# A hybrid mixer and MLP layer on one core: the Strassen sums of twelve weight pairs move from accumulating transfers to VectorE, and the branch and output weights are split where they are used

## The chip, the cores and the metric

One core of a Trainium2 chip runs the whole layer. The metric is the device time of one execution in microseconds. The kernel before was timed twice, 1608.06 and 1601.01 us, median 1604.53 us. Its profile is of a third execution.

## The reference

One layer on x of shape (1, 1024, 1024), float32. A combined projection feeds a pooling mixer and a stick-breaking attention of eight heads; two gates merge them, an output projection follows, and then an MLP of width 4096. Every projection is kept at nearly float32 precision.

```python
h = rmsnorm(x, g_pre_mix)
proj = h @ w_in                                  # [u_pool | q | k | v], 512 columns each
y_pool = multiscale_pool(u_pool, w_pool_mix, pool_scale) @ w_br_pool
o_sb = stick_breaking_attention(q, k, v)         # 8 heads of 64, strictly causal
y_sb = o_sb @ w_br_sb
gates = sigmoid(h @ w_gate + b_gate)             # 2048 columns
merged = gates[:, :1024] * y_pool + gates[:, 1024:] * y_sb
x = x + rmsnorm(merged @ w_out, g_post_mix)
h2 = rmsnorm(x, g_pre_mlp)
x = x + rmsnorm(square(relu(h2 @ w_up)) @ w_down, g_post_mlp)
```

The pooling mixer takes, for four groups of 128 channels, the mean over the last 2, 4, 8 or 16 positions minus the token itself, then a 128x128 map and a scale.

## The kernel before

Activations lie with channels on the 128 partitions and tokens along the free axis, in two halves of 512 tokens. Weights come in granules of 128x1024 (512 KB), an output tile of 128 columns with its eight blocks of the inner dimension. Each float32 operand is **split**: ScalarE casts it to a rounded high part, VectorE subtracts that to get the low part, and `mm3` forms a product from three TensorE matmuls (high by high, high by low, low by high). A split of a granule thus costs a copy on ScalarE and a subtraction on VectorE.

The stages follow one another:

- `phase_in` loads x, computes the norm, the pooling input u and the values v, and writes both to DRAM (`uscr`, `vscr`).
- `phase_project` computes queries, keys and gates with the Strassen-Winograd scheme: seven half products instead of eight, for **twelve pairs** of column tiles (`PAIRS`: four of queries and keys, eight of gates). For a pair with weight quarters a11, a12 (granule g1) and a21, a22 (granule g2) it needs, beside a1 = (a11, a12) and a22, the sums s3 = a21 + a22, s1 = a11 + a21, s2 = s3 + a11 and s4 = s2 + a12. In the kernel before, `sw_sums` makes them in DRAM: for three groups of four pairs, 24 transfers of 1 MiB on POOL's queue, each sum a plain transfer followed by an accumulating one, into `swscr`. `sw_weights` loads (s2, s4) and (s1, s3) from there, in rows of L524, and splits them.
- Within that stage two generators run in the background. `weight_sums` (L1204) makes the same kind of sums for the MLP's down weights, 32 transfers of 1 MiB on POOL's queue into `wscr`, issued a few at a time after the first result of each pair. `later` (L548) advances one step after each product: it prepares the values (`vscr` to `sscr`), pools the four groups (load of u L576, window sums L583, map by TensorE into dm, results to `yscr` L609), and at last takes the **branch and output weights**: sixteen granules are loaded (`hraw`, L612), split (L615 on ScalarE, L616 on VectorE), and both halves are stored to `hscr` (L618).
- Results of a pair go to DRAM on POOL's queue (`qscr`, `gscr`). Staging tiles for all this are four buffers of 512 KB in the pool `mx`, tags m0 to m3, taken in rotation by `staged`. The first two heads' queries and keys are loaded into the same four tags (L698 to L700).
- `phase_attention` runs eight heads for two halves of the queries: scores z, a scan on VectorE (L728), transposes, products with v. Between these it advances jobs: `job_pool` (branch product of the pooled path), `job_merge`, `job_out`. Their weights come by `prep`: for the branch and output weights, two loads of ready halves from `hscr` on SP's queue (L70); for the up weights, a load, a copy and a subtraction (L73 to L75). `weights(key)` prepares one key ahead, and the tiles whi and wlo have three buffers each.
- `phase_post` merges and projects the second half, and `phase_mlp` and `down` follow; they use Strassen sums too, made on VectorE for the up weights.

PSUM has eight banks, of which seven serve the pairs' products in rotation. The order of instructions on each engine is set by a scheduler; POOL, SP, VectorE and ScalarE each work through theirs in that order, so a row that waits holds up the rows behind it.

Of the kernel before, what the change touches and what calls it, by code (L numbers as in the profile page):

```python
# [32 lines left out]
P = 128  # L33
# [19 lines left out]
class Block:  # L53
# [10 lines left out]
    def prep(self, key, g, cols=None):  # L64
        nc = self.nc
        hi = self.wp.tile([P, 1024], F32R, name="whi", tag="whi", bufs=3)
        lo = self.wp.tile([P, 1024], F32R, name="wlo", tag="wlo", bufs=3)
        if cols is not None:
            for t, scr in zip((hi, lo), self.hscr[g - O_BR]):
                nc.sync.dma_start(t[:, cols].bitcast(F32), scr[:, cols])  # L70
        else:
            raw = self.wp.tile([P, 1024], F32, name="wraw", tag="wraw", bufs=2)
            nc.sync.dma_start(raw, self.w[g])  # L73
            nc.scalar.copy(hi, raw)
            self.last_lo = nc.vector.tensor_sub(lo, raw, hi.bitcast(F32)).ins  # L75
        self.prepped[key] = (hi, lo)
# [84 lines left out]
    def build(self):  # L161
# [25 lines left out]
        self.swscr = [[dp.tile([P, 4, 512], F32, name=f"swscr{n}_{q}") for q in range(4)] for n in range(3)]  # L187
        self.vscr = dp.tile([1 + P * NK, H], F32, name="vscr")
        self.sscr = [dp.tile([P, 1024], F32, name=f"sscr{t}") for t in range(NK)]
        self.hscr = [[dp.tile([P, 1024], F32, name=f"hscr{g}_{n}") for n in range(2)] for g in range(16)]  # L190
# [39 lines left out]
    def phase_in(self):  # L230
# [114 lines left out]
        def u_out(g, ps):  # L345
            for h, d in ps:
                s = evac()
                nc.vector.tensor_mul(s, d, self.rb[h])
                self.last_u = nc.gpsimd.dma_start(self.uscr[g][:, h * H : h * H + H], s)
# [23 lines left out]
        sums = self.sw_sums()  # L373
        for g in range(3):
            u_out(g, list(enumerate(dst[g])))
            if g == 0:
                with tc.issue_after(self.last_u.ins):
                    for _ in range(8):
                        next(sums)
# [21 lines left out]
        for _ in range(16):  # L401
            with tc.issue_after(self.last_u.ins):
                next(sums)
# [50 lines left out]
        gen = v_steps(1, (1, 2, 3, 0), banks)  # L454
        first = self.sw_weights(0)
# [42 lines left out]
    def sw_sums(self):  # L498

        nc = self.nc  # L500
        for n in range(3):
            g1, g2 = (self.w[g : g + 4] for g in self.sw_granules(n))
            a11, a12, a21, a22 = (g[:, :, c : c + 512].rearrange("e p n -> p e n") for g in (g1, g2) for c in (0, 512))
            s1, s2, s3, s4 = self.swscr[n]
            for out, x, y in ((s3, a21, a22), (s1, a11, a21), (s2, s3, a11), (s4, s2, a12)):
                yield nc.gpsimd.dma_start(out, x)
                yield nc.gpsimd.dma_start(out, y, accum_op=ALU.add)

    def sw_weights(self, i):
# [7 lines left out]
        for name, parts, where in (  # L517
            ("a1", (g1,), (self.wp, "w", 3)), ("sb", (s2, s4), (pool, f"s{i % 2}", 1)),
            ("sa", (s1, s3), (self.wp, "w", 3)), ("a22", (g2[:, 512:],), (pool, f"a{i % 2}", 1, 512)),
        ):  # L520
            raw = self.wp.tile([P, 1024], F32, name="wraw", tag="wraw", bufs=2)
            at = 0
            for p in parts:
                nc.sync.dma_start(raw[:, at : at + p.shape[-1]], p)  # L524
                at += p.shape[-1]
            w[name] = self.split_weights(raw[:, :at], *where)
# [21 lines left out]
    def later(self):  # L548

        nc = self.nc  # L550
        for t in range(NK):
            pair = self.staged([P, 2, H], F32, "vpair")
# [986 lines left out]
```

## Time and profile before

| | us |
|---|---|
| median of two runs | 1604.53 |
| profiled execution | 1606.4 |
| its span, first to last instruction | 1604.7 |
| TensorE busy | 1286.0 (80%) |
| VectorE busy | 945.3 (59%) |
| ScalarE busy | 615.6 (38%) |
| GpSimd (POOL) busy | 231.2 (14%) |
| DMA, share of 16 engines: queue of SP / of POOL | 39.0% / 31.9% |

The mean granted clock of TensorE was 0.902 of full speed. Transfers moved 359.58 MB. The profile has rows with the start of an instruction, its duration, its engine and line, what it writes and reads, and in brackets how long the engine was idle before and what ended that. SPq and POOL rows named DMA_DIRECT2D are issues of transfers, not the transfers. Rows of a window list the busy time of each engine in it, the granted clock, the mean busy share of the DMA engines and the rate in GB/s.

### The profile page before, as it was taken

How to read it: one execution, taken by the hardware profiler on the slowest of the kernel's cores; microseconds unless marked ns; L12 is line 12 of the kernel's file. 1: busy time of each engine (PE TensorE's matmuls, PEld its weight loads, DVE VectorE, ACT ScalarE, POOL GpSimd, SP SyncE). 2: the span in 40 equal slices, each digit the busy share in tenths (PEclk: the TensorE clock that was granted, in tenths of full speed). 3: DMA queues.
4: the chain of work that ended last, by engine and by line, in shares of the span. 5: the costliest groups of instructions: out<-in, count | busy, mean ns of one | idle time of the engine just before them, and what ended most of it. 6: DMA issues, size and time to landing. Idle time of an engine off the chain costs nothing. (4 is left out here: it accounts for less than half of the span.)

```text
span 1604.7 us, 16545 instructions
## 1 busy us (share of the span) xinstructions
PE 1286.0 (80%) x5707; PEld 1043.0 (65%) x5707; DVE 945.3 (59%) x1299; ACT 615.6 (38%) x982; POOL 231.2 (14%) x413
## 2 busy tenths in 40 slices
PE   9955885818790200788899999999999999999998
PEld 6844663616580100677777778878887788888888
DVE  8434553304461211568976478878777756576786
ACT  6223222304230111345555246655545544334443
POOL 1313222302121111121100111002111200000100
PEclk9976997868895555899999999999999999999999
DMA  5999999997967677676741686586655585465661
GB/s 189 290 267 258 271 338 287 289 228 236 256 229 264 224 250 245 193 221 183 234 126 67 232 318 216 186 288 213 215 184 177 189 296 196 171 216 180 235 254 53
DMA packets 126916, 359.58 MB, mean 224 GB/s; under 512 B 15024, under 2 KB 20144, under 8 KB 124560
## 3 DMA queue, kind: packets, MB, share of 16 engines
q1 hardware_dynamic: 78928, 202.77, 39.0%
q0 software_dynamic: 47760, 155.62, 31.9%
q8 instruction: 45, 0.74, 0.2%
q14 instruction: 39, 0.32, 0.1%
q10 hardware_dynamic: 144, 0.13, 0.0%
HBM read 270.39 MB, written 146.80 MB: 260 GB/s over the span
## 5 line engine op out<-in xcount | busy, mean ns | idle before, releaser
L105 PE MATMUL d<-blo,whi 128*128 128x512 f32 (+1 forms) x456 | 172.3, 378 | 0.0
L106 PE MATMUL d<-bhi,wlo 128*128 128x512 f32 (+1 forms) x456 | 171.9, 378 | 0.0
L104 PE MATMUL d<-bhi,whi 128*128 128x512 f32 (+1 forms) x456 | 168.7, 378 | 0.0
L722 PE MATMUL z<-kk,qq 128*128 128x256 f32 (+2 forms) x96 | 33.5, 358 | 90.9 <-DMA qq<-qscr 89.9
L104 PE MATMUL sw<-h_hi,whi 128*128 128x512 f32 x144 | 60.0, 418 | 54.1 <-ACT ev L416 31.5
L728 DVE TENSOR_TENSOR_SCAN T<-T,past 128x256 f32<-128x256 f32 (+3 forms) x96 | 90.0, 966 | 10.8 <-ACT T L727 9.6
L105 PEld LDWEIGHTS d<-blo,whi 128*128 128x128 f32 x456 | 85.7, 188 | 16.0
L106 PEld LDWEIGHTS d<-bhi,wlo 128*128 128x128 f32 x456 | 85.8, 188 | 15.8
L104 PEld LDWEIGHTS d<-bhi,whi 128*128 128x128 f32 x456 | 85.5, 188 | 16.1
L722 PEld LDWEIGHTS z<-kk,qq 128*128 128x128 f32 x96 | 18.3, 192 | 94.6 <-issue 90.3
L105 PE MATMUL d<-b_lo,whi 128*128 128x512 f32 x196 | 76.3, 389 | 0.0
L104 PE MATMUL d<-b_hi,whi 128*128 128x512 f32 x196 | 76.2, 389 | 0.0
L106 PE MATMUL d<-b_hi,wlo 128*128 128x512 f32 x196 | 75.6, 389 | 0.0
L616 DVE TENSOR_TENSOR hw<-hraw,hw 128x1024 fp32r<-128x1024 f32 x16 | 19.6, 1225 | 88.4 <-ACT hw L615 58.4
L104 PEld LDWEIGHTS sw<-h_hi,whi 128*128 128x128 f32 x144 | 28.9, 201 | 62.4 <-ACT ev L416 32.6
L753 DVE TENSOR_TENSOR alo<-at,ahi 128x512 fp32r<-128x512 f32 (+1 forms) x96 | 50.6, 548 | 28.2 <-ACT ahi L752 28.0
L1271 DVE TENSOR_TENSOR wlo<-slots_hi,whi 128x1024 fp32r<-128x1024 f32 x29 | 35.5, 1225 | 52.8 <-ACT whi L1269 52.7
L752 ACT CAST ahi<-at 128x512 fp32r<-128x512 f32 (+1 forms) x96 | 44.4, 482 | 54.8 <-PE at L744 37.7
L1269 ACT CAST whi<-slots_hi 128x1024 fp32r<-128x1024 f32 x29 | 30.5, 1052 | 83.2 <-PE d L105 70.2
L727 ACT ACTIVATE T<-z 128x256 f32<-128x256 f32 (+3 forms) x96 | 43.8, 496 | 42.6 <-PE z L725 25.1
L105 PE MATMUL sw<-h_lo,whi 128*128 128x512 f32 x144 | 59.3, 412 | 0.0
L106 PE MATMUL sw<-h_hi,wlo 128*128 128x512 f32 x144 | 58.0, 406 | 0.2
(416 smaller groups left out, 3573.2 us busy)
## 6 DMA issues: line engine op xcount, KB each, us to landing
wscr<-w POOLq DMA_DIRECT2D x24, 1024.0 KB, 20.9
wraw<-w SPq DMA_DIRECT2D x45, 512.0 KB, 5.4
ext_b<-ascr SPq DMA_DIRECT2D x40, 512.0 KB, 4.4
swscr<-w POOLq DMA_DIRECT2D x18, 1024.0 KB, 15.7
hscr<-hw POOLq DMA_DIRECT2D x32, 512.0 KB, 5.5
wraw<-swscr SPq DMA_DIRECT2D x48, 256.0 KB, 6.4
gt<-gscr POOLq DMA_DIRECT2D x32, 256.0 KB, 4.5
qq<-qscr SPq DMA_DIRECT2D x64, 128.0 KB, 5.0
```

Source lines behind the costliest of these rows:

```text
L104: nc.tensor.matmul(ps, wh, rh, start=first and i == 0, stop=False)
L105: nc.tensor.matmul(ps, wh, rl, start=False, stop=False)
L106: self.last_mm = nc.tensor.matmul(ps, wl, rh, start=False, stop=last and i == n - 1).ins
L616: nc.vector.tensor_sub(lo, raw, hi.bitcast(F32))
L722: m = nc.tensor.matmul(zz, qq[:, 0, tt], k[:, cols], start=True, stop=False)
L727: self.after = nc.scalar.activation(f, z[:, :n], AF.Sigmoid, scale=-1.0)
L728: nc.vector.tensor_tensor_scan(f[:, ::-1], f[:, ::-1], past[:, c : c + n][:, ::-1], 1.0 if top else tl[:, c + n : c + n + 1], ALU.mult, AL ...
L752: nc.scalar.copy(hi[:, c:], at[:, c:])
L753: nc.vector.tensor_sub(lo[:, c:], at[:, c:], hi[:, c:].bitcast(F32))
L1269: last_split[0] = nc.scalar.copy(hi, src).ins
L1271: last_split[1] = nc.vector.tensor_sub(lo, src, hi.bitcast(F32)).ins
```

## The change

Four things are edited. `sw_sums` and its DRAM tiles go: `sw_weights` loads the two granules of a pair, splits a1 and a22 from them, lets VectorE form the four sums in place (four additions of 128x512), and splits the tiles again as (s2, s4) and (s3 beside s1). The loaded tiles live longer, so a third buffer, wrawx, joins the two of wraw. The last part of `later` goes, with `hscr`: `prep` loads the columns it needs of the raw weights and splits them there, forty times (24 halves, 16 whole granules). To make room, c11, v and c22 have one buffer instead of two, `staged` uses two tags instead of four, and `later` gets two tags of its own with more steps between its loads and their use. Three down-weight sums are issued for each pair instead of four.

```diff
@@ def prep
-        if cols is not None:
-            for t, scr in zip((hi, lo), self.hscr[g - O_BR]):
-                nc.sync.dma_start(t[:, cols].bitcast(F32), scr[:, cols])
-        else:
-            raw = self.wp.tile([P, 1024], F32, name="wraw", tag="wraw", bufs=2)
-            nc.sync.dma_start(raw, self.w[g])
-            nc.scalar.copy(hi, raw)
-            self.last_lo = nc.vector.tensor_sub(lo, raw, hi.bitcast(F32)).ins
+        raw = self.wp.tile([P, 1024], F32, name="wraw", tag="wraw", bufs=2)
+        cols = slice(0, 1024) if cols is None else cols
+        nc.sync.dma_start(raw[:, cols], self.w[g][:, cols])
+        nc.scalar.copy(hi[:, cols], raw[:, cols])
+        self.last_lo = nc.vector.tensor_sub(lo[:, cols], raw[:, cols], hi[:, cols].bitcast(F32)).ins
@@ def phase_in
-        sums = self.sw_sums()
         for g in range(3):
             u_out(g, list(enumerate(dst[g])))
-            if g == 0:
-                with tc.issue_after(self.last_u.ins):
-                    for _ in range(8):
-                        next(sums)
...
-        for _ in range(16):
-            with tc.issue_after(self.last_u.ins):
-                next(sums)
@@ def sw_weights
-        g1, g2 = (self.w[g + e] for g in self.sw_granules(n))
-        s1, s2, s3, s4 = (s[:, e, :] for s in self.swscr[n])
+        raw = []
+        for g in self.sw_granules(n):
+            if next(self.raws) < 2 or self.sw_pools[1] is None:
+                t = self.wp.tile([P, 1024], F32, name="wraw", tag="wraw", bufs=2)
+            else:
+                t = self.sw_pools[1].tile([P, 1024], F32, name="wrawx", tag="wrawx")
+            nc.sync.dma_start(t, self.w[g + e])
+            raw.append(t)
+        r1, r2 = raw
+        a11, a12, a21, a22 = r1[:, :512], r1[:, 512:], r2[:, :512], r2[:, 512:]
         w = self.sw[i] = {}
+        w["a1"] = self.split_weights(r1, self.wp, "w", 3)
+        yield
         pool = self.sw_pools[i % 2]
...
+        w["a22"] = self.split_weights(a22, pool, f"a{i % 2}", 1, 512)
+        nc.vector.tensor_add(a22, a21, a22)
+        yield
+        nc.vector.tensor_add(a21, a11, a21)
+        nc.vector.tensor_add(a11, a11, a22)
+        nc.vector.tensor_add(a12, a12, a11)
+        yield
+        w["sb"] = self.split_weights(r1, pool, f"s{i % 2}", 1)
+        yield
+        w["sa"] = self.split_weights(r2, self.wp, "w", 3)
@@ def staged
-        return self.mx.tile(shape, dt, name=name, tag=f"m{self.turn % 4}")
+        return self.mx.tile(shape, dt, name=name, tag=f"m{self.turn % 2}")
@@ def later: vpair and vs take tags m2 and m3, one more step after the loads of a pair, two more after u
-        for g in range(16):
-            raw = self.staged([P, 1024], F32, "hraw")
-            nc.sync.dma_start(raw, self.w[O_BR + g])
-            yield
-            hi, lo = (self.staged([P, 1024], F32R, "hw") for _ in range(2))
-            nc.scalar.copy(hi, raw)
-            nc.vector.tensor_sub(lo, raw, hi.bitcast(F32))
-            for t, scr in zip((hi, lo), self.hscr[g]):
-                nc.gpsimd.dma_start(scr, t.bitcast(F32))
-            yield
@@ def phase_project
-            return pw.tile([P, H], F32, name=name, tag=name, bufs=2)
+            return pw.tile([P, H], F32, name=name, tag=name, bufs=1 + (name == "u"))
-            for _ in range(4):
+            for _ in range(3):
                 with tc.issue_after(done.ins):
                     next(self.wsums, None)
```

Three places show what moves. Line numbers of the changed kernel are its own, up to 22 lower.

POOL, from the end of the first projections to the first pair (vscr holds the values, vlast a small copy of them, qscr the first results, wscr the down weights' sums, swscr the pairs' sums). Before:

```order
L417 DMA vscr<-ev 128x512
L506 DMA swscr_1_151<-swscr_2_152 16x16384
L506 DMA swscr_1_155<-swscr_2_156 16x16384
L507 DMA swscr_3_149<-w 512x1x512
L507 DMA swscr_1_151<-w 512x1x512
L507 DMA swscr_1_155<-w 512x1x512
L417 DMA vscr<-ev 128x512 x3
L506 DMA swscr_3_153<-swscr_1_151 16x16384
L506 DMA swscr_3_157<-swscr_1_155 16x16384
L417 DMA vscr<-ev 128x512
L507 DMA swscr_3_153<-w 512x1x512
L507 DMA swscr_3_157<-w 512x1x512
```

With the change:

```order
L404 DMA vscr<-ev 128x512 x8
L466 DMA vlast<-vscr 64x8x1 x8
L532 DMA qscr_0_138<-qs 256x1x512
L1195 DMA wscr_0_126<-w 512x1x512
L1195 DMA wscr_1_127<-w 512x1x512
L1195 DMA wscr_2_128<-w 512x1x512
L549 DMA sscr_147<-vs 128x1024
L532 DMA qscr_2_140<-qs 256x1x512 x2
```

The stores of the values no longer stand between sums, and the first pair's first result is followed by three sums of the down weights.

VectorE, from the pooling of the fourth group (win, pq and u) to the first scans of attention (T); gt is a branch product. Before:

```order
L592 TENSOR_TENSOR win<-win,u 128x16
L597 TENSOR_TENSOR pq<-win,ph 128x1024
L604 SCALAR_TENSOR_TENSOR u<-dm,vt,win 128x512 x2
L616 TENSOR_TENSOR hw<-hraw,hw 128x1024 x4
L825 TENSOR_TENSOR gt<-gt,dbr 128x512
L616 TENSOR_TENSOR hw<-hraw,hw 128x1024 x12
L825 TENSOR_TENSOR gt<-gt,dbr 128x512
L728 SCALAR_TENSOR_TENSOR T<-T,past 128x512
```

With the change:

```order
L581 TENSOR_TENSOR win<-win,u 128x16
L586 TENSOR_TENSOR pq<-win,ph 128x1024
L593 SCALAR_TENSOR_TENSOR u<-dm,vt,win 128x512 x2
L804 TENSOR_TENSOR gt<-gt,dbr 128x512 x2
L72 TENSOR_TENSOR wlo<-wraw,whi 128x512
L707 SCALAR_TENSOR_TENSOR T<-T,past 128x512
```

The sixteen splits are gone from this place; one split of a branch weight stands there, and others stand among the scans behind it.

SP, where the fourth group's u is loaded, behind the loads of the values and of the third head's queries (qscr_2), with the change:

```order
L677 DMA qq<-qscr_2_140 64x512
L678 DMA qq<-qscr_2_140 64x512
L70 DMA wraw<-w 128x512
L563 DMA u<-uscr_137 128x1024
L679 DMA kk<-qscr_0_142 64x512 x4
L677 DMA qq<-qscr_0_138 64x512
```

The load of u keeps its place behind them; before, the loads of hraw and hscr followed it, and now the first heads' keys and queries do.

More of the change, by code (lines that the diff above doesn't have):

```diff
@@ L186, in build @@
         self.qscr = [[dp.tile([P, 2, 1024], F32, name=f"qscr{i}_{j}") for j in range(4)] for i in range(2)]
-        self.swscr = [[dp.tile([P, 4, 512], F32, name=f"swscr{n}_{q}") for q in range(4)] for n in range(3)]
         self.vscr = dp.tile([1 + P * NK, H], F32, name="vscr")
         self.sscr = [dp.tile([P, 1024], F32, name=f"sscr{t}") for t in range(NK)]
-        self.hscr = [[dp.tile([P, 1024], F32, name=f"hscr{g}_{n}") for n in range(2)] for g in range(16)]
         self.bscr = [[dp.tile([P, H], F32, name=f"bscr{e}_{h}") for h in range(2)] for e in range(8)]
@@ L348, in u_out @@
                 nc.vector.tensor_mul(s, d, self.rb[h])
-                self.last_u = nc.gpsimd.dma_start(self.uscr[g][:, h * H : h * H + H], s)
+                nc.gpsimd.dma_start(self.uscr[g][:, h * H : h * H + H], s)
         d2 = [self.dps.tile([P, H], F32, name="du", tag="d") for _ in range(2)]
@@ L454, in phase_in @@
         gen = v_steps(1, (1, 2, 3, 0), banks)
+        self.raws = itertools.cycle(range(3))
         first = self.sw_weights(0)
@@ L496, in sw_granules @@
         return a, a + (4 if n == 0 else 8)
[L498 to L507, printed above, removed]
     def sw_weights(self, i):
@@ L512, in sw_weights @@
         n, e = i // 4, i % 4
-        g1, g2 = (self.w[g + e] for g in self.sw_granules(n))
-        s1, s2, s3, s4 = (s[:, e, :] for s in self.swscr[n])
+        raw = []
[8 more added lines that the diff above has]
+        a11, a12, a21, a22 = r1[:, :512], r1[:, 512:], r2[:, :512], r2[:, 512:]
         w = self.sw[i] = {}
+        w["a1"] = self.split_weights(r1, self.wp, "w", 3)
+        yield
         pool = self.sw_pools[i % 2]
[L517 to L526, printed above, removed]
-            yield
+        w["a22"] = self.split_weights(a22, pool, f"a{i % 2}", 1, 512)
[8 more added lines that the diff above has]
+        w["sa"] = self.split_weights(r2, self.wp, "w", 3)
     def staged(self, shape, dt, name):
         self.turn += 1
-        return self.mx.tile(shape, dt, name=name, tag=f"m{self.turn % 4}")
+        return self.mx.tile(shape, dt, name=name, tag=f"m{self.turn % 2}")
     def result(self, kind, f, h, t, sign):
@@ L551, in later @@
         for t in range(NK):
-            pair = self.staged([P, 2, H], F32, "vpair")
+            p = self.mx.tile([P, 2, H], F32, name="vpair", tag="m2")
             for j in range(2):
-                nc.sync.dma_start(pair[:, j, :], self.vscr[t * P + j : t * P + j + P, :])
+                nc.sync.dma_start(p[:, j, :], self.vscr[t * P + j : t * P + j + P, :])
             yield
-            e = pair[:, 0, :]
-            nc.vector.tensor_sub(e, e, pair[:, 1, :])
+            yield
+            e = p[:, 0, :]
+            nc.vector.tensor_sub(e, e, p[:, 1, :])
             e = e.rearrange("p (h x) -> p h x", h=8)
-            v = self.staged([P, 8, P], F32R, "vs")
+            v = self.mx.tile([P, 8, P], F32R, name="vs", tag="m3")
             nc.scalar.copy(v[:, :, 0:64], e)
@@ L576, in later @@
             nc.sync.dma_start(u, self.uscr[g])
+            yield
+            yield
             yield
@@ L609, in later @@
                 nc.gpsimd.dma_start(scr.bitcast(F32), t)
-        for g in range(16):
-            raw = self.staged([P, 1024], F32, "hraw")
-            nc.sync.dma_start(raw, self.w[O_BR + g])
-            yield
-            hi, lo = (self.staged([P, 1024], F32R, "hw") for _ in range(2))
-            nc.scalar.copy(hi, raw)
-            nc.vector.tensor_sub(lo, raw, hi.bitcast(F32))
-            for t, scr in zip((hi, lo), self.hscr[g]):
-                nc.gpsimd.dma_start(scr, t.bitcast(F32))
-            yield
     def run(self, gen):
```

## The prediction

> **What bounds the kernel now.** I began with the slices of the page. From its third to its seventeenth forty-microsecond slice TensorE is far from full, and for four slices around the fourteenth it is nearly empty. From slice 18 on it is full. A change can only earn much in that hole.
>
> ```profile
> PE   9955885818790200788899999999999999999998
> DMA  5999999997967677676741686586655585465661
> ```
>
> So I cut the span at the places where the work changes: the first projections (0 to 99), the twelve pairs (99 to 486), the gap to the first attention score (486 to 649), attention (to 900), the merge and output products of the second half (to 960), the MLP.
>
> ```profile
> core 0: us, PE busy (x) PEld busy (x) DVE busy (x) ACT busy (x) POOL busy (x), PEclk, DMA share, GB/s
> 99.00:486.00 387.00, 261.32 (x1027) 206.60 (x1025) 165.90 (x230) 107.25 (x150) 83.65 (x121) 0.82 0.95 267
> 486.00:649.00 163.00, 11.90 (x27) 7.39 (x27) 29.95 (x32) 19.37 (x20) 22.82 (x43) 0.53 0.73 246
> 649.00:900.00 251.00, 230.07 (x1169) 187.37 (x1169) 185.22 (x282) 123.82 (x290) 31.49 (x86) 0.98 0.53 163
> 900.00:960.00 60.00, 55.13 (x225) 42.27 (x224) 38.62 (x60) 20.19 (x35) 10.73 (x20) 0.97 0.89 335
> 960.00:1605.00 645.00, 631.44 (x2858) 523.31 (x2857) 466.99 (x608) 304.82 (x424) 55.98 (x104) 1.00 0.60 204
> ```
>
> No compute engine is busy for more than 68% of the pairs' stage, while the DMA share is 0.95: transfers bound it. In the gap nothing is busy at all: a chain of small waits. After 649 TensorE leads, with VectorE at 74% in attention. The order of a wait's cause comes from the timeline: how a pair goes when transfers are light, what happens when accumulating transfers pile up, and how the gap is filled.
>
> ```profile
> 131.13 0.79 PE L104 MATMUL sw<-h_hi,whi 128*128 128x512 f32 x1 [29.39 <-ACT ev L416]
> 364.43 0.59 ACT L651 COPY u<-sw 128x512 f32<-128x512 f32 x1 [43.31 <-DMA gscr<-u]
> 447.23 0.57 ACT L651 COPY u<-sw 128x512 f32<-128x512 f32 x1
> 467.30 0.59 ACT L651 COPY u<-sw 128x512 f32<-128x512 f32 x1 [1.31 <-PE sw L106]
> 200.00:230.00 30.00, 23.92 (x95) 18.93 (x94) 12.26 (x17) 7.27 (x10) 5.91 (x9) 0.89 0.99 361
> 330.00:360.00 30.00, 0.00 (x0) 0.00 (x0) 0.00 (x0) 0.00 (x0) 1.68 (x3) 0.54 1.13 214
> ```
>
> The copy at L651 opens every pair, so two of them in a row give a pair that TensorE paces: 467.30 - 447.23 = 20.1 us. From 330 to 360 all engines stand still: the eight accumulating sums of the down weights (L1214) that were issued just before drain, at 214 GB/s with the share at 1.13, and the result of an earlier pair waits behind them (43.31 us). Plain traffic reaches 361 GB/s at a share of 0.99.
>
> **The pairs' stage (99 to 486).** What goes: those of the twelve pairs' sums that still ran here, and part of the weight loads.
>
> ```profile
> 101.18 0.50 POOL L506 DMA_DIRECT2D swscr<-swscr  x1 [4.77 <-DMA swscr<-w]
> 155.77 1.16 POOL L507 DMA_DIRECT2D swscr<-w  x1 [2.19 <-DMA swscr<-swscr]
> L1214 POOL DMA_DIRECT2D wscr<-w x16: 1151/1891/3557, 237.8 to 397.4; - x16
> wscr<-w POOLq DMA_DIRECT2D x24, 1024.0 KB, 20.9
> wraw<-w SPq DMA_DIRECT2D x45, 512.0 KB, 5.4
> wraw<-w SPq DMA_DIRECT2D x24, 256.0 KB, 6.5
> ```
>
> The first two rows are the first and the last of nine sums of 1 MiB issued after 99: 9.4 MB, five of them accumulating (5.2 MB). A pair's loads shrink from 1.84 MB (one granule of 512 KB, a half, and four quarter-megabyte sums) to 1.05 MB, some 9 MB in all. The stage moved 267 GB/s x 387 us = 103 MB; 85 MB stay, 16.8 MB of them the sixteen accumulating transfers of L1214. At the two rates above that is 16.8/0.214 = 78 us and 68/0.361 = 189 us, **267 us** of transfers. TensorE alone needs 12 x 20.1 = 241 us. The same sum for the kernel before gives 22/0.214 + 81/0.361 = 328 us, and it took 387, because a first-in-first-out queue also stalls TensorE where the transfers come unevenly: factor 1.18. So the new stage lies between 267 and 315 us. I take 290, the middle: the stall at 131 (29.39 us, the projection's results behind the pairs' sums in POOL's queue) goes, but the query and key pairs now hold their results in two buffers instead of four, and c11, v and c22 in one each, so a result store that lands late behind three sums of 1 MiB still stops VectorE. Saving **97 us** (72 to 120).
>
> VectorE gets four additions of 128x512 for each pair, 48 in all. A 128x512 operation on loaded data takes 0.69 us in the rows further down: 33 us on an engine busy for 166 us of the stage; 199 of 290 us leaves it off the bound. If that cover were gone it would cost at most these 33 us. The sums are no longer awaited from DRAM, but the raw tiles stay occupied until the last sum is split; three tiles rotate and the load is ahead by a pair, 20 us against 5.4 us of landing, so I cost it at nothing.
>
> **The gap (486 to 649).** Its rows in order of time:
>
> ```profile
> 484.31 7.17 SPq L680 DMA_DIRECT2D v<-sscr  x8
> 511.63 0.52 SPq L576 DMA_DIRECT2D u<-uscr  x1
> 516.67 1.22 DVE L583 TENSOR_TENSOR win<-u 128x1023 f32<-128x1023 f32 x1 [30.26 <-DMA u<-uscr]
> 532.16 0.54 POOL L609 DMA_DIRECT2D yscr<-u  x1 [0.25 <-DVE u L604]
> 537.12 0.53 POOL L674 DMA_DIRECT2D ylo<-yscr  x1
> 546.73 0.77 PE L104 MATMUL dbr<-yhi,whi 128*128 128x512 f32 x1 [16.38 <-DMA whi<-hscr]
> 639.23 1.22 DVE L616 TENSOR_TENSOR hw<-hraw,hw 128x1024 fp32r<-128x1024 f32 x1 [5.98 <-ACT hw L615]
> 640.48 0.45 SPq L698 DMA_DIRECT2D qq<-qscr  x1
> 649.42 1.08 PE L722 MATMUL z<-kk,qq 128*128 128x512 f32 x2 [89.94 <-DMA qq<-qscr]
> ```
>
> Two things fill it. First the pooling of the fourth group: its load of u stands on SP behind eight loads of v and twelve of queries and keys, is issued at 511.63, and the result goes out at 532.16 and comes back from 537.12. Then sixteen rounds of load, split and store of the branch and output weights, until 639.23; only then are the four buffers free for the first heads' queries, and 9 us later the first score runs. The change removes the rounds and nothing else: in its order the u load still stands behind the same v, query and key loads. What is late next is the store of the pooled u; when it has landed (537.12 - 486 = 51 us after the last product) the first head's transfers need what they needed before, 649.42 - 640.48 = 9 us. The gap becomes 60 to 64 us, I take 62: saving **101 us**. The bounds: 90, if the branch products, which now wait for a split, come in front of the scores; 110, if the lighter traffic lands u sooner.
>
> **Attention and the stage behind it.** Here the forty fetches of ready halves become loads, splits by ScalarE and VectorE.
>
> ```profile
> 134.11 0.62 ACT L1086 CAST a0hi<-wraw 128x512 fp32r<-128x512 f32 x1 [0.97 <-DMA wraw<-w]
> 134.77 0.69 DVE L1087 TENSOR_TENSOR a0lo<-wraw,a0hi 128x512 fp32r<-128x512 f32 x1 [2.35 <-ACT a0hi L1086]
> L75 DVE TENSOR_TENSOR wlo<-wraw,whi 128x1024 fp32r<-128x1024 f32 x17 | 20.8, 1221 | 7.6 <-ACT whi L74 7.6
> L74 ACT CAST whi<-wraw 128x1024 fp32r<-128x1024 f32 x17 | 17.9, 1053 | 18.1 <-PE d L105 9.8 <-DMA wraw<-w 6.0 <-PE du L105 2.3
> ```
>
> Three of the forty run in the gap. In attention there are thirteen halves and eight whole tiles: VectorE 13 x 0.69 + 8 x 1.22 = 18.7 us, ScalarE 13 x 0.62 + 8 x 1.05 = 16.5 us, on 185 and 124 of 251 us. Below nothing is not reached, above both in series, 35 us. I take **+9**: half of VectorE's share, since its scans hold TensorE for part of the stage only (230 of 251 us busy). From 900 to 960 eight halves and eight tiles add 15.3 us to VectorE's 38.6 of 60; TensorE waits 5 us there now, with the DMA share at 0.89, and half the bytes go. Bounds -5 and +15, I take **+3**. The MLP has no edit; its sums of the down weights end before attention in both.
>
> **The sum.** The profiled execution took 1606.4 us (its span 1604.7), 1.9 above the median of 1604.53. 1606.4 - 97 - 101 + 9 + 3 = **1420 us**.
>
> **A rule weighed.** The Trainium skill's page "DMA: Bandwidth & Descriptors", section "Bandwidth", gives 6.15 us or 341 GB/s for 1 MiB loaded by a software-generated transfer and no other price for one that accumulates. By it the 16.8 MB would be an estimated 49 us, not 78, the transfers 238 us, and TensorE would pace all pairs. The trace disagrees with its 214 GB/s, measured on DRAM to DRAM, where the page measured loads into SBUF.
>
> **The rivals.** (1) **TensorE paces every pair.** Accumulating transfers may be slow only because eight came in a row; now three a pair leave time for plain loads beside them. For it: the pairs from 447 on. Against: in the first pairs 8 MB a pair must move. The stage then takes 241: 1606.4 - 146 - 101 + 12 = 1371 us. (2) **The pairs' stage keeps its time**, because stores behind sums meet single buffers; for it, the 43.31 us of L651 came from exactly such a store with two buffers; against it, 18 MB less: 1420 + 97 = 1517 us. (3) **The gap keeps its time**: the change does not do what it says, since v, query and key loads and not the rounds hold the scores. Against it, the loads are all issued by 511.63 and the rounds end 9 us before the first score: 1420 + 101 = 1521 us. (4) **Slower: every split is waited for.** If SP, ScalarE and VectorE took the forty preparations in line with TensorE, 24 x (6.5 + 0.62 + 0.69) + 16 x (5.4 + 1.05 + 1.22) = 310 us: 1606.4 - 198 + 310 = 1718 us. It decides from 5 us each (198/40). Against it: seventeen splits by the same code waited 6.0 us in all for their loads.
>
> **Chances and range.** The forecast, 1385 to 1465, gets 0.72; rivals (1) 0.14, (2) 0.07, (3) 0.05, (4) 0.02. The low ends of the terms give 1606.4 - 120 - 110 - 5 = 1371; the high ends 1606.4 - 72 - 90 + 35 + 15 = 1494, which needs all four at once. I give 1374 to 1478, which takes in nearly all of the forecast and most of rival (1). A measurement of this kernel tells about 2% (32 us) from no change. All but rival (4) are faster by more: 0.97 faster, 0.01 within 2%, 0.02 slower.
>
> **What would show it.** Right: the first score near 450 us, no row of L616's kind between the last product and it, the u load of the fourth group some 26 us after the last product; the pairs' stage at a DMA share above 0.9 in its first half and pairs 20 us apart in its second; VectorE near 205 us in attention. Wrong: pairs 20 us apart from the first on (rival 1), copies of u waiting more than 20 us for a result store (2), more than 70 us from the last product to the first score (3), TensorE waiting for split weights in the branch and output products for more than a microsecond each (4).

## The result, and the profile after

The changed kernel took 1406.59 us (median of two runs) against 1604.53: a ratio of 0.877, with a 95% interval of 0.868 to 0.885. The forecast was 1420, its range 1374 to 1478. The profiled execution took 1407.21 us, its span 1405.5. The two rows of slices, to lay beside those of before:

```profile
PE   9998887899826988898989999999999999999998
DMA  5326999999965765620266668755565854656661
```

The hole in TensorE's row is now the twelfth slice and part of the thirteenth, where four stood before. The same stages by windows: pairs, gap, attention, the stage behind it, MLP.

```profile
core 0: us, PE busy (x) PEld busy (x) DVE busy (x) ACT busy (x) POOL busy (x), PEclk, DMA share, GB/s
97.00:377.00 280.00, 246.67 (x1024) 197.42 (x1023) 169.18 (x241) 97.14 (x137) 72.33 (x105) 0.95 0.94 277
377.00:438.00 61.00, 16.94 (x34) 8.60 (x33) 20.73 (x32) 6.79 (x9) 8.07 (x15) 0.53 0.73 244
438.00:684.00 246.00, 220.60 (x1128) 179.93 (x1127) 198.29 (x298) 136.46 (x305) 32.83 (x88) 0.98 0.45 130
684.00:764.00 80.00, 72.94 (x296) 58.03 (x295) 60.07 (x87) 37.76 (x61) 10.79 (x20) 0.94 0.59 205
764.00:1405.00 641.00, 628.20 (x2829) 519.98 (x2828) 462.34 (x601) 301.67 (x419) 56.19 (x104) 0.99 0.60 204
```

For all kernels below I cut each trace at the same five events: the first and the last product of the pairs, the first score, the last value product of attention, the first product of the MLP. The lengths between them, in us (the prediction's marks were round numbers near these; a "gap" below zero means that scores start before the pairs end):

| kernel | up to pairs | pairs | gap | attention | behind it | MLP | median |
|---|---|---|---|---|---|---|---|
| before | 98.9 | 385.3 | 165.2 | 241.2 | 71.5 | 642.6 | 1604.5 |
| after | 97.4 | 279.7 | 60.9 | 246.3 | 80.2 | 641.0 | 1406.6 |
| gap_part | 98.8 | 387.2 | 61.7 | 245.1 | 74.0 | 646.6 | 1516.5 |
| sums_part | 98.6 | 280.7 | 162.8 | 238.1 | 72.7 | 647.8 | 1500.1 |
| plain_sums | 98.9 | 257.9 | 63.2 | 246.4 | 80.5 | 640.0 | 1390.3 |
| no_acc_sums | 98.7 | 253.3 | 37.7 | 245.8 | 73.6 | 640.2 | 1350.9 |
| turning_tiles | 98.9 | 289.9 | 40.3 | 247.6 | 76.4 | 640.0 | 1396.9 |
| early_sums | 107.5 | 285.5 | 41.7 | 247.9 | 75.2 | 649.6 | 1408.1 |
| late_sums | 143.8 | 266.6 | 21.3 | 247.0 | 80.4 | 641.8 | 1401.8 |
| late_turning | 143.0 | 265.4 | -0.1 | 274.1 | 74.8 | 645.3 | 1405.3 |
| adds_twice | 98.4 | 316.9 | 43.3 | 247.7 | 73.2 | 648.0 | 1427.8 |
| attention_sums | 97.8 | 251.2 | 20.7 | 270.9 | 75.7 | 650.1 | 1368.4 |
| attention_turning | 98.4 | 249.6 | -0.1 | 289.5 | 80.9 | 647.5 | 1366.9 |
| spread_sums | 98.3 | 243.6 | 43.7 | 267.3 | 80.5 | 640.4 | 1375.5 |

So the change took 105.6 us from the pairs and 104.3 from the gap, and gave back 5.1 in attention and 8.7 behind it. The kernel before was timed again beside each group of later runs; its medians lay between 1604.2 and 1606.1 us, so times of different groups may be compared to within about 2 us. The length "behind it" needs care: in the kernel before (and in sums_part) the last 22 matmuls of that stage run only after the first one of the MLP, until 968.4 us; in the changed kernel (and in gap_part) none does. At 0.24 us each they are an estimated 5.3 us, counted behind attention after the change and in the MLP before it.

How the pairs go now, by the timeline of the copy that opens each (L630, L651 before): the sixth opens 50 us after the fifth; from the eighth on they are 18 to 24 us apart. What held the sixth stands in the rows behind them: six accumulating sums (L1193) go out on GpSimd's queue within 8 us, then the store of a block of values (sscr). The values have one tile for that store (vs), and ScalarE waits 19.91 us for the store to land before it casts the next block and comes to the pair's copy.

```profile
199.68 0.59 ACT L630 COPY u<-sw 128x512 f32<-128x512 f32 x1 [3.76 <-DVE qs L529]
249.59 0.59 ACT L630 COPY u<-sw 128x512 f32<-128x512 f32 x1 [0.81 <-DVE ks L529]
297.90 0.57 ACT L630 COPY u<-sw 128x512 f32<-128x512 f32 x1
319.45 0.56 ACT L630 COPY u<-sw 128x512 f32<-128x512 f32 x1
...
202.91 3.61 POOL L1193 DMA_DIRECT2D wscr<-w  x3 [0.42 <-issue]
207.05 3.59 POOL L1193 DMA_DIRECT2D wscr<-w  x3
208.94 2.26 POOL L549 DMA_DIRECT2D sscr<-vs  x1
246.90 0.62 ACT L547 CAST vs<-vpair 128x512 fp32r<-128x512 f32 x1 [19.91 <-DMA sscr<-vs]
```

And the gap, in order of time (timeline, three engines and the queue of SP together):

```profile
394.61 0.54 POOL L598 DMA_DIRECT2D yscr<-u  x1 [0.25 <-DVE u L593]
402.43 0.33 SPq L563 DMA_DIRECT2D u<-uscr  x1
409.14 1.22 DVE L572 TENSOR_TENSOR win<-u 128x1023 f32<-128x1023 f32 x1 [14.82 <-DMA u<-uscr]
424.63 0.54 POOL L598 DMA_DIRECT2D yscr<-u  x1 [0.25 <-DVE u L593]
438.01 1.16 PE L701 MATMUL z<-kk,qq 128*128 128x512 f32 x3
```

No round of load, split and store is left. The load of the fourth group's u is issued 25.3 us after the last product (402.43 - 377.1; announced: some 26), its pooling ends with the store at 424.63, and the first score follows 13 us later.

### The profile page after: what moved, and what is told of

Same layout as the page of the kernel before. It is cut to its first block, busy times and chain, and to the rows that moved or that the text cites. A ratio compares the mean times of both kernels' runs of the same rounds, so it can differ in the third digit from the quotient of the medians.

```text
span 1405.5 us, 16309 instructions
## 1 busy us (share of the span) xinstructions
PE 1279.6 (91%) x5707; PEld 1038.3 (74%) x5707; DVE 982.5 (70%) x1371; ACT 626.3 (45%) x1006; POOL 193.1 (14%) x357
## 5 line engine op out<-in xcount | busy, mean ns | idle before, releaser
L71 ACT CAST whi<-wraw 128x1024 fp32r<-128x1024 f32 (+1 forms) x57 | 49.6, 872 | 73.0 <-PE dbr L102 32.6
L72 DVE TENSOR_TENSOR wlo<-wraw,whi 128x1024 fp32r<-128x1024 f32 (+1 forms) x57 | 56.6, 994 | 27.9 <-ACT whi L71 26.5
L103 PE MATMUL d<-b_hi,wlo 128*128 128x512 f32 x196 | 74.8, 389 | 0.0
L1248 ACT CAST whi<-slots_hi 128x1024 fp32r<-128x1024 f32 x29 | 30.5, 1051 | 83.2 <-PE d L102 66.6
L732 DVE TENSOR_TENSOR alo<-at,ahi 128x512 fp32r<-128x512 f32 (+1 forms) x96 | 50.6, 548 | 20.7 <-ACT ahi L731 20.0
L1248 ACT CAST whi<-slots_lo 128x1024 fp32r<-128x1024 f32 x27 | 28.5, 1054 | 73.5 <-PE d L102 58.2
L1250 DVE TENSOR_TENSOR wlo<-slots_lo,whi 128x1024 fp32r<-128x1024 f32 x27 | 33.0, 1223 | 35.5 <-ACT whi L1248 35.3
L723 PE MATMUL at<-eye,T 128*128 128x128 f32 x288 | 47.9, 275 | 10.8 <-DVE alo L732 10.7
```

Source lines behind the costliest of these rows:

```text
L71: nc.scalar.copy(hi[:, cols], raw[:, cols])
L72: self.last_lo = nc.vector.tensor_sub(lo[:, cols], raw[:, cols], hi[:, cols].bitcast(F32)).ins
L103: self.last_mm = nc.tensor.matmul(ps, wl, rh, start=False, stop=last and i == n - 1).ins
L723: t = nc.tensor.transpose(at[:, r * P : r * P + P], a[r][:, s * P : s * P + P], self.eye)
L732: nc.vector.tensor_sub(lo[:, c:], at[:, c:], hi[:, c:].bitcast(F32))
L1248: last_split[0] = nc.scalar.copy(hi, src).ins
```

## The experiments

Two theories stood against each other at each place. Mine: the two parts are separate, transfers at two rates bound the pairs, a chain of pooling bounds the gap. Against it: the parts hide or expose each other; places in queues and buffers, not bytes, hold the pairs.

**One part alone, twice.** gap_part is the kernel before with this edit (and without the rounds in the generator):

```diff
-        if cols is not None:
-            for t, scr in zip((hi, lo), self.hscr[g - O_BR]):
-                nc.sync.dma_start(t[:, cols].bitcast(F32), scr[:, cols])
...
+        nc.sync.dma_start(raw[:, cols], self.w[g][:, cols])
+        nc.scalar.copy(hi[:, cols], raw[:, cols])
+        self.last_lo = nc.vector.tensor_sub(lo[:, cols], raw[:, cols], hi[:, cols].bitcast(F32)).ins
```

> The kernel before, with only the branch and output weights split at their use (no rounds of load, split and store ahead of attention). Theory (the two parts are separate and add): the gap loses about 104 us, attention and the stage behind it gain 14, the pairs' stage keeps its 385 us: 1606 - 104 + 14 = 1516, between 1500 and 1532. Rival A (the fourth group's load and the loads of v and queries hold the first score once the rounds are gone, because the transfers ahead are as heavy as before): the gap falls only to about 100 us, 1555. Rival B (the rounds' own traffic slowed the end of the pairs' stage): the pairs' stage falls too, below 1490.

Measured 1516.46, ratio 0.944 (0.941 to 0.947). sums_part is the other half: the changed kernel with the sixteen rounds and the fetches of ready halves put back, in the four tiles' own turn.

```diff
+            tags = [f"m{(3 * g + k) % 4}" for k in range(3)]
+            raw = self.mx.tile([P, 1024], F32, name="hraw", tag=tags[0])
...
+            hi, lo = (self.mx.tile([P, 1024], F32R, name="hw", tag=t) for t in tags[1:])
```

> The kernel after, with the sixteen rounds ahead of attention put back (branch and output weights fetched ready from DRAM again), so that only the twelve pairs' sums are changed. Theory (additive): 1407 + 104 - 14 = 1497, between 1480 and 1512, pairs' stage 280 us as in the changed kernel. Rival (the rounds are paid for only as far as transfers are congested, and with 9 MB less ahead of them they run faster): a gap of 120 us instead of 163 and 1455.

Measured 1500.12, ratio 0.935 (0.931 to 0.938). The two savings, 87.9 and 104.2, add to 192.1 where the whole change saved 197.9; the rivals of both runs are out. The table shows it stage by stage: gap_part has the pairs of before (387.2) and the gap of after (61.7), sums_part the reverse (280.7 and 162.8). The pair of runs also prices the splits in both surroundings: with them attention and the stage behind it are 3.9 and 2.5 us longer (gap_part against before), or 8.2 and 7.5 (after against sums_part), the second figure of each pair with those 22 matmuls.

**What bounds the pairs.** plain_sums makes sixteen transfers plain, no_acc_sums leaves them out (first and second diff, both in weight_sums):

```diff
-                    self.nc.gpsimd.dma_start(out[q], a, accum_op=ALU.add)
+                    self.nc.gpsimd.dma_start(out[q], a)
```

```diff
-                if add:
-                    self.nc.gpsimd.dma_start(out[q], a, accum_op=ALU.add)
-                else:
+                if not add:
                     self.nc.gpsimd.dma_start(out[q], a)
```

> The kernel after, with the sixteen accumulating transfers of the down weights' sums made plain copies of the same size and place (the down products' weights are then not the sums). Theory (two rates, 214 GB/s for accumulating and 361 for plain): 16.8 MB take 46 us instead of 78, the transfers of the pairs' stage 215 instead of 247, so TensorE paces the stage at about 250 instead of 280 us, and poolings that start earlier shorten the gap by some 5: 1372, between 1360 and 1385. Rival A (accumulating costs no more per byte): no change, 1400 to 1412. Rival B (what costs is the place in POOL's queue, a result behind 1 MiB of anything): a third of the gain at most, 1395.

> The kernel after, with the sixteen accumulating transfers of the down weights' sums left out (so these sums are not formed; the sixteen plain ones stay). Theory (transfers bound the rest of the pairs' stage): 169 us of transfers remain, TensorE paces all pairs, stage about 247 us, gap 50 instead of 61: 1364, between 1350 and 1375. Rival (the single buffers of c11, v and c22 and of the value tiles hold the pairs, not the transfers): stage still above 270 us and 1395 or more.

Measured 1390.29 (0.866, 0.864 to 0.868) and 1350.92 (0.841, 0.839 to 0.844). The windows of the pairs' stage, plain_sums first, then no_acc_sums:

```profile
99.00:357.00 258.00, 241.89 (x1023) 195.68 (x1022) 173.78 (x248) 97.65 (x136) 64.36 (x104) 0.97 0.86 303
```

```profile
99.00:352.00 253.00, 242.12 (x1030) 196.37 (x1029) 186.33 (x270) 103.58 (x143) 57.82 (x98) 0.97 0.71 254
```

The last three columns are the clock, the DMA share and the rate. The share falls from 0.94 to 0.86 and 0.71, TensorE is busy for 242 of 258 and 253 us. So transfers did bind what was left of the stage, and an accumulating one costs more than a plain one of the same size: 21.8 us of the stage for sixteen, where the two rates gave 32. That price is not spread over the sixteen. Some 16 of the 21.8 us lie between the fifth and the sixth opening copy (49.9 us apart in the changed kernel, 34.2 in plain_sums), behind the six sums of 203 us. While they move, the changed kernel's rate is 243 GB/s at a share of 1.08; in plain_sums the same stretch runs at 359 GB/s at 0.99, and the store behind them costs ScalarE 3.71 us instead of 19.91:

```profile
203.00:246.00 43.00, 34.75 (x143) 27.54 (x141) 16.85 (x22) 9.70 (x13) 11.25 (x13) 0.94 1.08 243
```

```profile
203.00:230.00 27.00, 25.38 (x103) 20.11 (x103) 16.29 (x21) 9.14 (x13) 8.48 (x13) 0.94 0.99 359
230.14 0.62 ACT L547 CAST vs<-vpair 128x512 fp32r<-128x512 f32 x1 [3.71 <-DMA sscr<-vs]
```

The total of plain_sums fell by 16 and not by the announced 34, outside the theory's range: the stage gave some 8 us less than announced, and the gap, which was to shorten by 5, stayed (63.2). It lies between theory and rival B, and the rows above bear out a part of rival B: the place behind 1 MiB transfers in GpSimd's queue matters. Leaving the sums out (no_acc_sums, inside its range) took 55.7 us, of which only 26.4 are in the pairs and 23.2 in the gap: poolings that are no longer delayed. Single buffers by themselves hold nothing, since they are the same in all three kernels; behind sums in the queue one of them, vs, turned a late landing into the longest stall of the stage. Rate, place in the queue and single tile act together there, and no run has a second vs tile to price it alone.

**What holds the gap.** In turning_tiles a group's u goes to the tile that its predecessor's ph leaves, not to the one whose store must land first:

```diff
+        tags = [0, 1, 2, 3]
         for g in range(4):
-            u = whole(0, name="u")
+            tu, t1, t2, tq = tags
+            u = whole(tu, name="u")
...
-            ph, pq = whole(3 - n, F32R, "ph"), whole(3, F32R, "pq")
+            th = t1 + t2 - n
+            tags = [th, tq, tu, n]
+            ph, pq = whole(th, F32R, "ph"), whole(tq, F32R, "pq")
```

> The kernel after, with the four tiles of the pooling groups taken in turn: a group's load of u goes to the tile of the group before's ph, which is free after its two products, and not to the tile that waits for the store of u to land. Theory (the gap is the chain of four poolings, each load held by the single tile of u until the store before it has landed): each of three loads comes 8 to 10 us earlier, the first score 15 to 25 us earlier: 1387, between 1380 and 1394. Rival (the loads are held by the place of the steps between the pairs' products, or by transfers): no change, 1402 to 1410.

Measured 1396.85 (0.870, 0.867 to 0.873): half of what was expected. SP's own waits for the four loads, of the changed kernel (in all, then between 399 and 404 us alone), and of this one:

```profile
SPq L563 <- DMA yscr<-u: 23.3, 3, 12.2
SPq L563 <- DMA yscr<-u: 2.7, 1, 2.7
```

```profile
SPq L565 <- PE dm L103: 7.3, 2, 3.9
```

The tile held the second and the third load (8.4 and 12.2 us). The fourth, the only one in the gap, waited for it for 2.7 us. It is issued at 388.01 instead of 402.43 mainly because it now stands ahead of the eight loads of values in SP's order, and the gap falls by 20.6 us. But the pairs' stage is 10.2 us longer, and the trace shows most of that: TensorE waits there for the casts of two pooled groups, 10.4 us where the changed kernel has 1.6. A group's window sums now take the tile that the store holds, so VectorE waits for the store in SP's stead. Rows of turning_tiles:

```profile
PE dm L101 <- ACT ph L589: 10.4, 2, 5.5
372.17 1.22 DVE L574 TENSOR_TENSOR win<-win 128x1022 f32<-128x1022 f32 x1 [9.00 <-DMA yscr<-u]
377.40 0.80 PE L101 MATMUL dm<-ph,wm 128*128 128x512 f32 x1 [5.46 <-ACT ph L589]
388.01 0.60 SPq L565 DMA_DIRECT2D u<-uscr  x1
388.66 10.82 SPq L663 DMA_DIRECT2D v<-sscr  x8
```

**Sums of the down weights elsewhere.** early_sums issues twelve of the thirty-two in the first projections, and two instead of three for each pair.

```diff
             u_out(g, list(enumerate(dst[g])))
+            if g == 0:
+                for _ in range(8):
+                    with tc.issue_after(self.last_u.ins):
+                        next(self.wsums)
...
+        for _ in range(4):
+            with tc.issue_after(self.last_u.ins):
+                next(self.wsums)
```

> The kernel after, with twelve of the thirty-two transfers of the down weights' sums (8 plain, 4 accumulating) issued during the first projections, and two instead of three for each pair. Theory (transfers bound the pairs' stage; the first 97 us have room at 137 GB/s): 8.4/0.361 + 4.2/0.214 = 43 us of transfers leave the stage, which becomes TensorE-paced at 255 instead of 277 us, gap 45 to 55: 1370, between 1355 and 1385. Rival (the first results stand in POOL's queue behind them, as in the kernel before at 131 us, 29 us): 1395 to 1410.

Measured 1408.06 (0.877, 0.874 to 0.881): the rival. The pairs' stage does fall to a share of 0.79, and from its first opening copy to its end it takes 254 us (263 in the changed kernel). But that copy comes at 139.06 instead of 114.37. The window of the stage, the copy, and the waits of this kernel between 100 and 160 us:

```profile
107.00:393.00 286.00, 245.47 (x1027) 197.82 (x1028) 192.18 (x280) 108.58 (x153) 66.98 (x103) 0.95 0.79 235
```

```profile
139.06 0.58 ACT L637 COPY u<-sw 128x512 f32<-128x512 f32 x1
```

```profile
POOL vscr L411 <- ACT ev L410: 45.4, 5, 20.9
ACT ev L410 <- DMA vscr<-ev: 18.9, 2, 16.5
```

The stores of the values stand behind sums in GpSimd's queue, as at 131 us in the kernel before. That waiting is a matter of the queue's order, and no sum of bytes contains it.

late_sums and late_turning were to issue all thirty-two in attention, behind each head's scores (late_turning with the tiles in turn as well).

```diff
+                for _ in range(2):
+                    with tc.issue_after(self.after.ins):
+                        next(self.wsums, None)
                 out = self.att_steps(h, g, [a[i] for i in rows[::-1]])
```

> The kernel after, with all thirty-two transfers of the down weights' sums issued in attention, two behind each of the sixteen heads' score groups, and none during the pairs. Theory (what is bound by transfers is only the pairs' stage; attention moves 130 GB/s and has room for 124 us of transfers in 246): pairs' stage 248 us and gap 41 us as in the run without accumulating sums, attention and post together +10: 1360, between 1345 and 1375. Rival (the gates' loads and stores in POOL's queue stand behind 1 MiB transfers, and the branch products hold TensorE): attention +40 or more, 1390 to 1420.

> The two edits together: sums of the down weights in attention and the pooling groups' tiles taken in turn. Theory: they add as far as poolings are still the end of the gap: late sums' time minus 10, 1350. Rival (without the sums' traffic the poolings end in time and something else, the loads of the first heads, holds the first score): same as with late sums alone.

Neither ran so. The instruction they were tied to (self.after, the last sigmoid) is ScalarE's, and it held back nothing on GpSimd; the trace of late_sums has the first eight sums at the very start:

```profile
L1195 POOL DMA_DIRECT2D wscr<-w x8: 793/1182/1595, 4.1 to 8.4; - x8
L1193 POOL DMA_DIRECT2D wscr<-w x16: 1151/1164/1250, 18.1 to 148.2; - x16
```

So these two are runs with all sums beside the first projections: 46 us are lost there (143.8 against 97.4), 13 won in the pairs, 40 in the gap; 1401.77 (0.873, 0.871 to 0.876) and, with the turned tiles, 1405.28 (0.876, 0.873 to 0.879). They say nothing on their expectations.

attention_sums does it: each sum is queued behind a store or load that GpSimd itself issues for the branch products.

```diff
-            for _ in range(3):
-                with tc.issue_after(done.ins):
-                    next(self.wsums, None)
...
-        nc.gpsimd.dma_start(self.bscr[e][h], t)
+        self.some_sums(nc.gpsimd.dma_start(self.bscr[e][h], t), 1)
```

> The kernel after, with the thirty-two transfers of the down weights' sums in attention, each queued on GpSimd behind a store or a load of the branch products there (one behind each of sixteen, two behind each of eight), and none during the pairs. Theory (the sums' transfers bind in the pairs' stage alone; attention moves 130 GB/s of 361): pairs' stage 250 us, gap 35 to 40, attention and post together no more than +12: 1352, between 1342 and 1368. Rival (the branch products' loads and stores in the same queue stand behind 1 MiB transfers, and TensorE waits for them in order): attention +40 us or more, 1385 to 1420.

> The same, with the pooling groups' tiles taken in turn as well. Theory (in the run with those tiles alone the gap fell by 21 us and the pairs' stage rose by 10, since transfers still bound it; without the sums there is nothing to give back): 5 to 20 us less than with the sums in attention alone: 1338. Rival (without the sums the poolings are early, and the loads of the first heads into the same four tiles end the gap): same time within 4 us.

Measured 1368.42 (0.852, 0.849 to 0.855) and 1366.85 (0.852, 0.849 to 0.854). They beat the changed kernel by 2.7 and 2.8%. The first lies just outside the theory's range: the pairs came as expected (251.2), the gap below it (20.7), but attention is 25 us longer and the MLP 9, where 12 were the most expected for attention and the stage behind it. Windows of attention_sums, the pairs and the two parts of attention:

```profile
98.00:349.00 251.00, 242.30 (x1034) 197.77 (x1033) 188.42 (x272) 104.87 (x144) 47.82 (x82) 0.97 0.55 189
370.00:550.00 180.00, 156.13 (x731) 125.82 (x731) 137.67 (x209) 90.47 (x214) 52.14 (x100) 0.89 1.07 313
550.00:641.00 91.00, 82.96 (x404) 67.25 (x403) 62.14 (x90) 45.90 (x93) 10.97 (x20) 0.96 0.54 147
```

The share is 0.55 in the pairs and 1.07 in the first 180 us of attention: the load on the transfers has moved there. What it costs there shows as slower products more than as waits. TensorE is busy for 239 us of attention where it was 221 in the changed kernel, for about as many matmuls (1134 and 1129), with a granted clock of 0.89 in the first 180 us where it was 0.97; its idle time grows by 6.5 us. Why the clock is lower these runs do not show. With the turned tiles the gap disappears (-0.1) and attention takes the same time back (289.5): the rival's time, within 2 us. A first score stands right behind the pairs there, but a later one waits 11 us, while SP still issues the first heads' queries, until 384:

```profile
382.29 0.76 PE L702 MATMUL z<-kk,qq 128*128 128x512 f32 x1 [11.08 <-issue]
```

The profile names no releaser for that wait, so that these loads end it, as the rival said, is likely and not shown.

spread_sums puts the first eight back to the pairs and one instead of two behind each merge product.

```diff
             done = self.result(kind, f1, 0, c11, 1.0)
+            if i < 8:
+                self.some_sums(done, 1)
...
-            self.some_sums(self.last_in, 2)
+            self.some_sums(self.last_in, 1)
```

> The kernel after, with the eight first plain transfers of the down weights' sums in the first eight pairs (one each), and the other twenty-four in attention, one behind each of the sixteen pool products' stores and one behind each of eight merge products' loads. Theory (transfers may be put wherever a stage has room; with all in attention its first 180 us had a DMA share of 1.03 to 1.08 and attention rose by 25): 8 MB at 361 GB/s fit beside the pairs, which stay at 252, gap 25, attention 258 to 264: 1360, between 1352 and 1368. Rival (the price of a transfer is the same in either place, since what the pairs lose attention gains): 1366 to 1374, no better than with all of them in attention.

Measured 1375.48 (0.858, 0.856 to 0.861), worse than either said. The pairs were never shorter (243.6), but the gap is 43.7. SP's queue shows a reason, here and in no_acc_sums. In spread_sums:

```profile
343.95 8.20 SPq L658 DMA_DIRECT2D v<-sscr  x8
354.26 0.45 SPq L677 DMA_DIRECT2D qq<-qscr  x1
382.08 0.59 SPq L677 DMA_DIRECT2D qq<-qscr  x1
```

```profile
385.62 1.30 PE L700 MATMUL z<-kk,qq 128*128 128x512 f32 x3 [22.12 <-DMA qq<-qscr]
```

All eight loads of the values go out ahead of the first heads' queries, which are issued until 382. In attention_sums five of the eight stand behind most of them, and the score comes 20.7 us after the pairs:

```profile
365.86 4.06 SPq L656 DMA_DIRECT2D v<-sscr  x5
```

A kernel with spread sums and the queries ahead of the values was not tried, so this is read from the traces.

**VectorE's additions.** adds_twice puts one more operation of the same size behind each of the 48.

```diff
         nc.vector.tensor_add(a22, a21, a22)
+        self.same(a22)
...
+    def same(self, x):
+        self.nc.vector.scalar_tensor_tensor(out=x, in0=x, scalar=1.0, in1=x, op0=ALU.mult, op1=ALU.max)
```

> The kernel after, with one more VectorE operation of 128x512 on the same tile behind each of the pairs' 48 additions (a product with one and a maximum, which changes no value). Theory (VectorE is busy 169 of 280 us in the pairs' stage and the raw weights are ahead of their use, so the additions lie beside other work): 48 x 0.68 = 33 us more of work, no more than 5 of them seen: 1402 to 1412. Rival (load, four additions and the last split are a chain that TensorE waits for in every pair): most of the 33 us appear, 1430 or more.

Measured 1427.77 (0.888, 0.885 to 0.892), 21 us more: between the theory (1402 to 1412) and its rival (1430). My theory is out. The pairs alone are 37 us longer (316.9); the gap fell by 17.6, since the fourth u was loaded at the same time as in the changed kernel (403.0 and 402.4 us) while the pairs ended later. Of the 37, 16 are TensorE's products taking longer (busy 262.5 against 246.7 us, granted clock 0.89 against 0.95) and 21 are waits. SP's waits for the tile of a raw weight from 97 to 415 us, after and then with the added operations (L496 is the load of a pair's weights):

```profile
SPq L496 <- DVE wlo L1066: 62.0, 8, 11.4
SPq L496 <- DVE s0lo L1066: 24.9, 6, 8.1
```

```profile
SPq L496 <- DVE wlo L1073: 75.8, 9, 20.3
SPq L496 <- DVE s0lo L1073: 51.3, 6, 13.2
```

The next pair's load waits for the split behind the additions, 40 us more in sum: the tile stays occupied longer and the load goes out later. The other path is direct. ScalarE's casts of the sums wait for the operation in front of them, and TensorE for these casts: 16.7 us in the changed kernel, 26.5 with the added operations. How much goes by which path no run shows; one with a fourth raw tile would.

```profile
PE sw L101 <- ACT whi L1065: 16.7, 6, 5.5
```

```profile
PE sw L101 <- ACT whi L1072: 26.5, 7, 8.2
```

## Why the prediction was right, point by point

- **Pairs, 290 forecast, 279.7 measured (bounds 267 to 315).** The bound was right: less traffic made the stage shorter, and less again made it TensorE's (253.3, 243.6; forecast 241 for TensorE alone). The number is partly luck, as errors on both sides met. The two rates gave too high a price to accumulating: 32 us for the sixteen, 21.8 in the stage. The traffic fell by more than was counted, to 277 GB/s x 280 us = 77.6 MB and not 85. Put into the same sum, it gives 16.8/0.214 + 60.8/0.361 = 247 us; the stage took 1.13 times that, before 1.18. And a factor for the whole stage hides that the largest single loss sits at one place, the store behind six sums: the kind of late store that the text named, but of the values, not of a pair's result.
- **The additions at nothing.** This step failed. They are not hidden with room to spare: doubled, they cost 21 us of the kernel and 37 of the stage, more than the 33 that the text named as the most. The first 48 are on the path as well: in the changed kernel ScalarE's casts of weights wait 13.5 us in eight waits for an addition (L507), and some of TensorE's 16.7 us stand behind these casts. What the first 48 cost by themselves was not measured. The raw tiles that "stay occupied until the last sum is split" were the very cover that I counted on.
- **The gap, 62 forecast, 60.9 measured, by the reason given, with a second one close behind.** The rounds went and nothing else did, as said; gap_part gives 61.7 by itself. There the load of the fourth u goes out 27.9 us after the last product, right behind the loads of values and queries on SP, while the store that frees its tile was issued long before, at 490.11:

```profile
490.11 0.54 POOL L605 DMA_DIRECT2D yscr<-u  x1 [0.25 <-DVE u L600]
...
513.92 0.52 SPq L572 DMA_DIRECT2D u<-uscr  x1
```

  In the changed kernel the same loads stand ahead of it. SP is through with them at 399.7, 22.6 us after the last product, and then waits 2.7 us more for the tile. The forecast did not name the tile; it set the last tenth of the 25.3 us.

```profile
399.17 0.53 SPq L70 DMA_DIRECT2D wraw<-w  x1
```

- **Attention +9 and the stage behind it +3, measured +5.1 and +8.7.** The sum (12 against 13.8, of which the 22 matmuls are some 5) is near, its parts are less so. VectorE has 198 of 246 us, near the 205 announced. Behind attention TensorE waits twice for a split, once at length, and once for the merge:

```profile
PE d L103 <- DVE wlo L72: 4.4, 2, 4.0
PE d L101 <- ACT mg_hi L826: 2.7, 1, 2.7
```

  That is 7.1 us of waits; before, it waited 4.9 us for transfers. The other part is time at work, 73.1 us where it was 66.6: the 22 matmuls more, some 5.3 us, and a granted clock of 0.94 where it was 0.98. Without these matmuls the stage is some 3.4 us longer, near the forecast of 3.
- **The rule that was weighed.** The Trainium skill's page "DMA: Bandwidth & Descriptors", section "Bandwidth", has one price for 1 MiB and no other for one that accumulates. plain_sums disagrees: the same sixteen transfers without accumulating took 16 us less of the whole and landed sooner (median of the sixteen 12.0 us from issue, with accumulating 20.8). The estimate of 49 us was worked out from the rate alone. The two figures of that row do not fit each other: 1 MiB in 6.15 us is 170 GB/s, and sixteen times 6.15 us are an estimated 98 us, so the page gives no firm price here.
- **The rivals.** TensorE did not pace every pair (rival 1): the sixth opens 50 us after the fifth. It does without the sums. Rivals 2 and 3 are out by the stages. But the mechanism of 2, a store behind sums that meets a single buffer, made the longest stall of the pairs (19.91 us on ScalarE, at 246.90), and the mechanism of 3, loads on SP that hold the first score, is what its row in spread_sums shows. Splits waited for one after another (rival 4) do not occur.

## What to carry to other kernels

Cut a trace at the same events in every version, and compare stages: here the parts of a change added to within 6 us, while an edit in one stage was often paid back in the next (20.6 won in the gap, 10.2 lost in the pairs; 20.8 and 18.6 between attention_sums and attention_turning). In these runs a transfer that was moved was cheap only where the share of DMA left room and nothing urgent stood behind it in its queue: the same thirty-two sums cost 46 us beside the first projections, and left 38 less on the whole when moved into attention. And an engine at 60% may still sit on the path, if what it does releases the tile that the next load waits for.

## What was not expected of the hardware

- Sixteen accumulating transfers of 1 MiB from DRAM to DRAM took a median of 20.8 us to land, plain ones of the same size and place 12.0. They cost 21.8 us more of the pairs' stage, some 16 of them at the one place where six went out together.
- In the gap of the changed kernel a product of 128x512 shows 0.63 us (0.39 in full work), with a granted clock of 0.53 over that window. In turning_tiles the products behind TensorE's wait of 5.46 us (377.40) show 0.63 us each, and 0.39 again from 380.48 on. In these rows a wait costs more than its own length.
- The MLP, whose code is the same in all, took 640 to 650 us. In attention_sums TensorE waits there for VectorE's splits for 12.3 us, in the changed kernel for 5.6. What sets this was not found.
